# A decoder step whose first norm is summed on VectorE alone, behind two weight tiles, with its product four blocks later

## The chip, the cores and the metric

One core of a Trainium2 chip runs one launch of the whole step. The metric is the device time of that launch in microseconds (us), the median of several runs. The engines are TensorE (PE in the profile, with its weight loads shown as PEld), VectorE (DVE), ScalarE (ACT), GpSimd (POOL) and SyncE (SP), which here issues nearly all DMAs. Each engine works through its own instructions in the order in which they stand in its queue; semaphores tie the queues together.

## The reference

Two layers of a decoder, for a prompt of 256 positions and eight single-token samples. These 264 columns go through everything together.

```python
def rmsnorm(x, g):
    y = xf * lax.rsqrt(jnp.mean(xf * xf, axis=-1, keepdims=True) + EPS)
    return (y * g).astype(x.dtype)

def moba_gmlp_mixer(x, pos, past_kv, norm_g, w_in, ...):      # layer 0
    h = rmsnorm(x, norm_g)
    z = h @ w_in
    q, k, v, bu, bv = jnp.split(z, ...)
    ...
```

Layer 0 is followed by a ConvFFN, layer 1 by another, and a last rmsnorm ends the step. Only the start of layer 0 is touched here: the first rmsnorm and the product with `w_in`.

## The kernel before

Everything is kept transposed: features on the 128 partitions, the 264 columns along the free axis. A matrix product is made of **blocks** of 128x128 weights, and each block takes three TensorE matmuls, since weights and activations are split into a rounded high half (`wh`, `xg_h`) and a low half (`wl`, `xg_l`): high by high, high by low, low by high. All weights of the step are one stream of blocks in the order of their use. Eight blocks make one **weight tile**: tile n holds the blocks 8n to 8n+7, so tile 4 holds blocks 32 to 39, tile 5 blocks 40 to 47, tile 8 blocks 64 to 71. For each tile ScalarE writes the high half (`wh<-raw`, 128x1024) and VectorE the low half (`wl<-raw,wh`). The raw weights arrive by DMA in **chunks**: the first three tiles come together with `x` in `xw`, chunks 3, 4 and 5 are one tile each (tiles 3, 4, 5), and from chunk 6 on a chunk is two tiles of 1 MB in all (chunk 6 is tiles 6 and 7, chunk 7 tiles 8 and 9, chunk 8 tiles 10 and 11). Raw chunks from 6 on share three buffers, `wh` and `wl` have four each.

The norm is not applied ahead of the product: `z` is computed from `x` times the gain, and the factor R = rsqrt(mean square + eps) of each column is multiplied in when a finished output leaves its PSUM bank. To get R, ScalarE squares the eight slices of `x` into two tiles `sq0[0]` and `sq0[1]` of four slices; `sum0` folds each of them to one slice with two additions (128x528, then 128x264); one more addition (`summed`) joins the two; a TensorE product with a matrix of ones (`ns_n`) sums over the partitions; and ScalarE takes logarithm and exponential (`R_n`, in `rstd_of`). In the kernel before, GpSimd folds `sq0[0]` and VectorE `sq0[1]`.

The first product of layer 0, `in0`, has 20 outputs. The first six (four of `bv`, two of `q`) are accumulated side by side in blocks 0 to 47, the others one after the other with eight blocks each: q2 in blocks 48 to 55, q3 in 56 to 63, k0 in 64 to 71. Products take PSUM banks from a pool of four in turn (`psm`); q0, q1 and q2 (blocks 4, 5 and 48) take theirs from another pool. So q3, at block 56, takes the bank of the first `bv`, and k0, at block 64, that of the second. An output that is finished before R exists is put on a list (`held`), and `norm0`, which makes R, writes out those held.

The order of instructions comes from two sources. What goes through `keep` (`tc.keep_in_program_order`) stays in the order of the program on its engine: the start of the program, all TensorE work, and all of SP's loads through `late`. The rest is placed by a scheduler; `behind(i, j)` only tells it that instruction i comes after j. In the main loop `run`, `split(t)` prepares weight tiles up to three ahead (two for a few) and asks for the raw chunks of the tile and of the two chunks after it; `blk(b, f)` runs the hook f once b blocks have been written. `kload` hooks at blocks 24, 32, 40 and so on each put two loads of the sample's key cache (`K`, 256 KB each) into SP's queue. `whole(tt)` prepares a tile ahead of that loop, and does not ask for further chunks; the next call of `split` goes on from the first tile that isn't there yet.

Of the kernel before, what the change touches and what calls it, by code (L numbers as in the profile page):

```python
# [207 lines left out]
def tile_decoder_step(ctx: ExitStack, tc: tile.TileContext, a):  # L208
    nc = tc.nc
    v, s, g = nc.vector, nc.scalar, nc.gpsimd  # L210
    fixed = [False]

    class TensorE:

        @staticmethod
        def keep(i):
            return tc.keep_in_program_order(i) if fixed[0] else i
# [21 lines left out]
    def f4(name, shape=(P, 4, T), dt=F32):  # L239
        return up.tile(list(shape), dt, tag="u", name=name)  # L240
# [46 lines left out]
    def wtiles(tt):  # L287
        return [p.tile([P, 8, WP], F32R, tag=f"w{x}", name=f"w{x}{tt}")[:, :, :P] for p, x in ((wsh, "h"), (wsl, "l"))]

    def by_block(w):  # L290
        return w.rearrange("p (b c) -> p b c", c=P)

    def raw(ci):
        if ci not in raws:
            n = _CHUNKS[ci] * P
            r = f4(f"raw{ci}", (P, n)) if ci < C8 else rawp.tile([P, n], F32, tag="raw", name=f"raw{ci}")
            o = (coff[ci] - NB1) * P * P
            raws[ci] = r
            late(r, a["w"][o:o + P * n].rearrange("(p f) -> p f", p=P))
        return raws[ci]  # L300
# [7 lines left out]
    def split(t):  # L308
        for tt in range(len(splits), min(t + (2 if t in NEAR else LOOK), NT - 1) + 1):
            ci = chunk_of[tt]  # L310
            for c in range(ci, min(ci + 3, len(_CHUNKS))):
                raw(c)
            o = (tt * 8 - coff[ci]) * P
            src = by_block(raws[ci][:, o:o + 8 * P])
            h, l = splits[tt] = wtiles(tt)
            i = s.activation(h, src, AF.Copy)  # L316
            if R0 and tt < 9:
                behind(i, last[0])
            if tt == 17:
                behind(i, turned["a", 3])  # L320
            if tt == 18:
                behind(i, turned["t", 3])
            i = v.tensor_tensor(l, src, h.bitcast(F32), ALU.subtract)  # L323
            if tt == 5:
                behind(i, summed)
            if tt == 13:
                behind(i, turned["k", 1])
            if tt in (15, 16):
                behind(i, turned["p", 2 * tt - 29])
        return splits[t]  # L330
# [3 lines left out]
    def run(order, rhs, evac, hooks=None):  # L334
# [5 lines left out]
        for m, k in order:  # L340
            i = pos[0]
            pos[0] += 1
            h, l = split(i // 8)
            c = i % 8
            if m not in ps:
# [122 lines left out]
    def behind(i, j):  # L468

        tc.add_manual_dep(i.ins, j.ins.name, mybir.DependencyInfo(mybir.DependencyClass.NoSync, mybir.DependencyReason.DATA), reason="order")  # L470
# [275 lines left out]
    def whole(tt, pieces=1):  # L746
        h, l = splits[tt] = wtiles(tt)
        ci = chunk_of[tt]
        o = (tt * 8 - coff[ci]) * P
        src = by_block(raws[ci][:, o:o + 8 * P])  # L750
        n = 8 // pieces
        for c in range(0, 8, n):
            keep(s.activation(h[:, c:c + n], src[:, c:c + n], AF.Copy))  # L753
            keep(v.tensor_tensor(l[:, c:c + n], src[:, c:c + n], h[:, c:c + n].bitcast(F32), ALU.subtract))  # L754
# [10 lines left out]
    sq0 = [f4(f"sq0_{i}") for i in range(2)]  # L765
# [4 lines left out]
    def square(m):  # L770
        keep(s.activation(sq0[m // 4][:, m % 4, :], xin[m], AF.Square))
# [18 lines left out]
    def sum0(e, q):  # L790

        keep(e.tensor_tensor(q[:, 0:2, :], q[:, 0:2, :], q[:, 2:4, :], ALU.add))
        keep(e.tensor_tensor(q[:, 0, :], q[:, 0, :], q[:, 1, :], ALU.add))

    sum0(g, sq0[0])
    whole(4, 2)
    square(4)
    keep(s.activation(sq0[1][:, 1:4, :], first[-1][2], AF.Square))
    sum0(v, sq0[1])
    summed = keep(v.tensor_tensor(sq0[1][:, 0, :], sq0[0][:, 0, :], sq0[1][:, 0, :], ALU.add))  # L800
    rope = f4("rope")
    held = []
# [214 lines left out]
    blk = lambda b, f, *x: hk.at(b / 8 - 1, f, *x)  # L1017
# [12 lines left out]
        blk(112 + 6 * n, drip_of(vload, 2))  # L1030
    for m in range(0, KD, 2):
        blk(120 + 4 * m, late_x, m)
    blk(39, norm0)
    blk(40, masks)
    blk(44, gm_first)
    blk(64, late, VEC, a["vec"])
    blk(72, sm_q)
    for t in range(4):
# [205 lines left out]
    blk = lambda b, f, *x: hk.at(b / 8 - 1, f, *x)  # L1244
# [109 lines left out]
```

## Time and profile before

| what | value |
|---|---|
| median of 3 runs | 584.74 us (584.72 to 584.82) |
| the profiled execution's own time | 584.81 us |
| its span, first to last instruction | 583.0 us |
| granted TensorE clock, mean | 0.999 |
| busy: PE, DVE, ACT, POOL | 577.8, 421.7, 345.9, 113.3 us |
| DMA moved | 122.40 MB, mean 210 GB/s |

Times in the trace are counted from the start of the span; 1.8 us of the execution lie around it. A row of the timeline gives start, duration, engine, line, operation and tiles, with the number of merged instructions (x2) and, in square brackets, the idle time before it and who ended it. Buffer numbers are left out there, so that all weight tiles read `wl<-raw,wh`.

### The profile page before, as it was taken

To read this page: it belongs to the slowest core of one execution; us is meant where nothing else is said; L and a number is where in the kernel's file an instruction comes from. 1 tells how busy PE (TensorE), PEld (TensorE's weight loads), DVE (VectorE), ACT (ScalarE), POOL (GpSimd) and SP (SyncE) were. 2 spreads that over 40 slices of the span, in tenths; PEclk is the share of its full clock that TensorE was granted. 3 is DMA by queue.
4 is the path that set the end of the run, shared out by engine and by line. 5 is a ranking of instruction groups with operands and counts; after the bars stand their busy time and mean duration, and the time that the engine had idled before them with its cause. 6 is when DMAs were issued, how large, how long until landed. Compare 5 with 4: busy or idle time off the path is not lost.

```text
span 583.0 us, 12325 instructions
## 1 busy us (share of the span) xinstructions
PE 577.8 (99%) x4913; PEld 563.5 (97%) x4913; DVE 421.7 (72%) x743; ACT 345.9 (59%) x618; POOL 113.3 (19%) x108
## 2 busy tenths in 40 slices
PE   9999999999999999999999999999999999999997
PEld 8998979999999999999999897999999999999996
DVE  6999766877777777665659685688777777765442
ACT  7848945775555556654454576667656564665442
POOL 2410031222223232210110000122232323221010
PEclk9999999999999999999999999999999999999999
DMA  8998973455554545795567855254545454546501
GB/s 332 373 358 285 402 256 114 178 183 180 164 198 156 205 153 209 266 399 209 183 230 270 307 203 182 83 208 155 207 149 211 148 209 153 200 171 223 209 4 74
DMA packets 27707, 122.40 MB, mean 210 GB/s; under 512 B 3330, under 2 KB 4226, under 8 KB 16258
## 3 DMA queue, kind: packets, MB, share of 16 engines
q1 hardware_dynamic: 27648, 121.62, 58.3%
q8 instruction: 38, 0.62, 0.4%
q14 instruction: 19, 0.16, 0.1%
q10 hardware_dynamic: 2, 0.00, 0.0%
HBM read 117.65 MB, written 3.96 MB: 209 GB/s over the span
## 4 chain that ended last, share of the span: by engine, by line
PE 96%; ACT 1%; DMA 1%; DVE 1%; SPq 0%; issue 0%; DVEq 0%
PE mm L220 88%; PE sc L220 1%; PE pv_l L220 1%; PE pav L220 1%; PE pt L223 1%; DMA xw<-in_xw 1%; PE S L220 1%; PE Z L220 1%; DVE wl L754 0%; ACT xg_h L424 0%; PE pf L220 0%; PE vtp_v L223 0%; SPq L389 0%; ACT wh L753 0%; ACT wh L741 0%; PE y L223 0%
## 5 line engine op out<-in xcount | busy, mean ns | idle before, releaser
L323 DVE TENSOR_TENSOR wl<-raw,wh 128x1024 fp32r<-128x1024 f32 x179 | 219.5, 1230 | 63.8 <-ACT wh L316 63.5
L316 ACT ACTIVATE wh<-raw 128x1024 fp32r<-128x1024 f32 x179 | 187.7, 1051 | 79.6 <-PE mm L220 73.8
L220 PE MATMUL mm<-xg_f_h,wh 128*128 128x264 f32 x704 | 197.8, 281 | 0.0
L220 PE MATMUL mm<-xg_f_h,wl 128*128 128x264 f32 x704 | 197.8, 281 | 0.0
L220 PE MATMUL mm<-xg_f_l,wh 128*128 128x264 f32 x704 | 197.5, 280 | 0.0
L220 PEld LDWEIGHTS mm<-xg_f_h,wh 128*128 128x128 f32 x704 | 131.9, 187 | 0.0
L220 PEld LDWEIGHTS mm<-xg_f_h,wl 128*128 128x128 f32 x704 | 131.9, 187 | 0.0
L220 PEld LDWEIGHTS mm<-xg_f_l,wh 128*128 128x128 f32 x704 | 131.9, 187 | 0.0
L616 POOL TENSOR_TENSOR wk<-wk 128x264 f32<-128x264 f32 x44 | 66.5, 1513 | 193.5 <-DVE wk L615 147.3
L220 PE MATMUL mm<-a_h,wl 128*128 128x264 f32 x352 | 98.9, 281 | 0.0
L220 PE MATMUL mm<-a_h,wh 128*128 128x264 f32 x352 | 98.9, 281 | 0.0
L220 PE MATMUL mm<-a_l,wh 128*128 128x264 f32 x352 | 98.7, 280 | 0.0
L220 PEld LDWEIGHTS mm<-a_l,wh 128*128 128x128 f32 x352 | 66.0, 187 | 0.0
L220 PEld LDWEIGHTS mm<-a_h,wl 128*128 128x128 f32 x352 | 65.9, 187 | 0.0
L220 PEld LDWEIGHTS mm<-a_h,wh 128*128 128x128 f32 x352 | 65.9, 187 | 0.0
L473 ACT ACTIVATE a_h<-wk 128x264 fp32r<-128x264 f32 x44 | 18.6, 423 | 73.6 <-POOL wk L616 73.6
L474 DVE TENSOR_TENSOR a_l<-wk,a_h 128x264 fp32r<-128x264 f32 x44 | 19.2, 437 | 42.1 <-ACT a_h L473 42.1
L220 PE MATMUL mm<-xg_h,wl 128*128 128x264 f32 x160 | 42.7, 289 | 0.0
L220 PE MATMUL mm<-xg_h,wh 128*128 128x264 f32 x160 | 42.3, 286 | 0.0
L220 PE MATMUL mm<-xg_l,wh 128*128 128x264 f32 x160 | 41.6, 281 | 0.0
L220 PE MATMUL mm<-xg_n_h,wl 128*128 128x264 f32 x128 | 36.9, 288 | 0.0
L220 PE MATMUL mm<-xg_n_h,wh 128*128 128x264 f32 x128 | 36.0, 281 | 0.0
(271 smaller groups left out, 903.8 us busy)
## 6 DMA issues: line engine op xcount, KB each, us to landing
raw<-in_w SPq DMA_DIRECT2D x89, 1024.0 KB, 4.9
K<-in_kt SPq DMA_DIRECT2D x32, 256.0 KB, 7.0
V<-in_vp SPq DMA_DIRECT2D x32, 256.0 KB, 5.9
raw<-in_w SPq DMA_DIRECT2D x3, 512.0 KB, 6.6
xw<-in_xw SPq DMA_DIRECT2D x3, 388.0 KB, 5.4
X<-in_x SPq DMA_DIRECT2D x4, 264.0 KB, 6.9
out_y<-y SPq DMA_DIRECT2D x3, 256.0 KB, 2.3
out_k<-k SPq DMA_DIRECT2D x1, 528.0 KB, 7.5
```

The source lines that it names most:

```text
L220: return self.keep(nc.tensor.matmul(*x, **k))
L223: return self.keep(nc.tensor.transpose(*x, **k))
L316: i = s.activation(h, src, AF.Copy)
L323: i = v.tensor_tensor(l, src, h.bitcast(F32), ALU.subtract)
L473: s.activation(h, src, AF.Copy)
L474: v.tensor_tensor(l, src, h.bitcast(F32), ALU.subtract)
L616: g.tensor_tensor(A, A, C, ALU.mult)
```

## The change

Tile 4 is split in one piece instead of two. Tile 5 is now split with `whole` as well, ahead of the main loop, and after it VectorE does all the additions of the first norm, in the order `sq0[0]`, `sq0[1]`, `summed`. What the scheduler is told to keep behind `summed` is now the low half of tile 6 instead of tile 5. The hook with the norm's product and R moves from after 39 blocks to after 43, the masks from 40 to 44, the first gelu from 44 to 47.

```diff
             i = v.tensor_tensor(l, src, h.bitcast(F32), ALU.subtract)
-            if tt == 5:
+            if tt == 6:
                 behind(i, summed)
...
-    sum0(g, sq0[0])
-    whole(4, 2)
+    whole(4)
     square(4)
     keep(s.activation(sq0[1][:, 1:4, :], first[-1][2], AF.Square))
-    sum0(v, sq0[1])
+    whole(5)
+    for q in sq0:
+        sum0(v, q)
     summed = keep(v.tensor_tensor(sq0[1][:, 0, :], sq0[0][:, 0, :], sq0[1][:, 0, :], ALU.add))
...
-    blk(39, norm0)
-    blk(40, masks)
-    blk(44, gm_first)
+    blk(43, norm0)
+    blk(44, masks)
+    blk(47, gm_first)
```

Lines after the edit move down by one. In the rows below, numbers tell buffers apart within one kernel and differ between the two.

VectorE's queue from tile 4 on. In the kernel before, `wl_350` is tile 4, `wl_427`, `wl_487` and `wl_491` are tiles 5, 6 and 7; `mm_370` and `mm_380` are the accumulators of the first `bv` and of q0.

```order
L754 TENSOR_TENSOR wl_350<-raw_136,wh_349 128x4x128 x2
L792 TENSOR_TENSOR sq_1_312<-sq_1_312 128x528
L793 TENSOR_TENSOR sq_1_312<-sq_1_312 128x264
L800 TENSOR_TENSOR sq_1_312<-sq_0_311,sq_1_312 128x264
L323 TENSOR_TENSOR wl_427<-raw_157,wh_426 128x8x128
L323 TENSOR_TENSOR wl_487<-raw_159,wh_486 128x8x128
L323 TENSOR_TENSOR wl_491<-raw_159,wh_490 128x8x128
L807 TENSOR_TENSOR rope<-ropecs,R_n_517 128x264
L808 SCALAR_TENSOR_TENSOR rope<-ropecs,R_n_517 128x264
L841 TENSOR_TENSOR bv_366<-mm_370,R_n_517 128x264
```

In the changed kernel `wl_354` is tile 5 (it stands just ahead of these rows, behind tile 4), `wl_485` and `wl_489` are tiles 6 and 7, `wl_522` is tile 8, and `mm_372` and `mm_382` are the accumulators of the first `bv` and of q0.

```order
L792 TENSOR_TENSOR sq_0_311<-sq_0_311 128x528
L793 TENSOR_TENSOR sq_0_311<-sq_0_311 128x264
L792 TENSOR_TENSOR sq_1_312<-sq_1_312 128x528
L793 TENSOR_TENSOR sq_1_312<-sq_1_312 128x264
L801 TENSOR_TENSOR sq_1_312<-sq_0_311,sq_1_312 128x264
L323 TENSOR_TENSOR wl_485<-raw_159,wh_484 128x8x128
L323 TENSOR_TENSOR wl_489<-raw_159,wh_488 128x8x128
L323 TENSOR_TENSOR wl_522<-raw_480,wh_521 128x8x128
L834 STREAM_SHUFFLE rz_q_555<-mm_382 128x264
L808 TENSOR_TENSOR rope<-ropecs,R_n_536 128x264
L809 SCALAR_TENSOR_TENSOR rope<-ropecs,R_n_536 128x264
L842 TENSOR_TENSOR bv_368<-mm_372,R_n_536 128x264
```

Five additions instead of three now stand between tile 5's low half and tile 6's, and tile 8's low half and a shuffle stand ahead of everything that uses R.

ScalarE's queue, from tile 6 on. Before, with `wh_486` and `wh_490` for tiles 6 and 7, `wh_537` and `wh_582` for tiles 8 and 9:

```order
L316 ACTIVATE wh_486<-raw_159 128x8x128
L316 ACTIVATE wh_490<-raw_159 128x8x128
L462 ACTIVATE R_n_517<-ns_n_515,epst 128x264
L463 ACTIVATE R_n_517<-R_n_517 128x264
L817 ACTIVATE onesr<-ones 128x128
L819 ACTIVATE mask_361<-CST 128x127 x2
L316 ACTIVATE wh_537<-raw_424 128x8x128
L960 ACT_TABLE_LOAD
L316 ACTIVATE wh_582<-raw_424 128x8x128
```

In the changed kernel, with `wh_484`, `wh_488`, `wh_521` and `wh_580` for tiles 6, 7, 8 and 9:

```order
L316 ACTIVATE wh_484<-raw_159 128x8x128
L316 ACTIVATE wh_488<-raw_159 128x8x128
L316 ACTIVATE wh_521<-raw_480 128x8x128
L462 ACTIVATE R_n_536<-ns_n_534,epst 128x264
L463 ACTIVATE R_n_536<-R_n_536 128x264
L818 ACTIVATE onesr<-ones 128x128
L820 ACTIVATE mask_363<-CST 128x127 x2
L961 ACT_TABLE_LOAD
L316 ACTIVATE wh_580<-raw_480 128x8x128
```

Tile 8's high half has moved from behind R and the masks to a place ahead of R's logarithm.

SP's queue after the last register load. Before, with `raw_424` for chunk 7 (tiles 8 and 9) and `raw_484` for chunk 8:

```order
L282 DMA raw_424<-in_w 128x2048
L282 ISA
L282 DMA K_0_454<-in_kt 128x512
L282 ISA
L282 DMA K_0_454<-in_kt 128x512
L282 ISA
L282 DMA K_2_481<-in_kt 128x512
L282 ISA
L282 DMA K_2_481<-in_kt 128x512
L282 DMA raw_484<-in_w 128x2048
```

In the changed kernel, with `raw_480` for chunk 7 and `raw_482` for chunk 8:

```order
L282 ISA
L282 DMA K_0_450<-in_kt 128x512
L282 ISA
L282 DMA K_0_450<-in_kt 128x512
L282 ISA
L282 DMA K_2_477<-in_kt 128x512
L282 ISA
L282 DMA K_2_477<-in_kt 128x512
L282 DMA raw_480<-in_w 128x2048
L282 DMA raw_482<-in_w 128x2048
```

Chunk 7 was asked for when the main loop first prepared tile 5; with tile 5 done ahead of that loop, it is asked for with tile 6, after the hooks of blocks 24 and 32 have put four `K` loads into the queue. TensorE's matmuls stay as they were, but for the product `ns_n`, which stands four blocks later.

## The prediction

> **What bounds the kernel now.** I read the page first: the span, the busy times and the chain that ended last.
>
> ```profile
> span 583.0 us, 12325 instructions
> PE 577.8 (99%) x4913; PEld 563.5 (97%) x4913; DVE 421.7 (72%) x743; ACT 345.9 (59%) x618; POOL 113.3 (19%) x108
> PE 96%; ACT 1%; DMA 1%; DVE 1%; SPq 0%; issue 0%; DVEq 0%
> ```
>
> TensorE is busy for 99% of the span and carries 96% of the chain. A change can therefore win only the microseconds in which TensorE pauses, and it loses whatever new pause it makes, since hardly anything later is idle enough to take a delay back. So I looked for the pauses at the place of the change: the waits of the first 80 us name one, the product of the norm, on TensorE's loads and on its matmuls.
>
> ```profile
> PEld ns_n L220 <- DVE sq L800: 0.4, 1, 0.4
> PE ns_n L220 <- DVE sq L800: 0.2, 1, 0.2
> ```
>
> TensorE's timeline there, matmul by matmul (start, duration):
>
> ```profile
> 18.62 0.28 PE L220 MATMUL mm<-xg_h,wl 128*128 128x264 f32 x1
> 19.09 0.71 PE L220 MATMUL ns_n<-sq,ones 128*128 128x264 f32 x2 [0.19 <-DVE sq L800]
> 19.45 0.48 PE L220 MATMUL mm<-xg_h,wh 128*128 128x264 f32 x1
> 19.77 0.28 PE L220 MATMUL mm<-xg_l,wh 128*128 128x264 f32 x1
> 20.25 0.37 PE L220 MATMUL mm<-xg_h,wl 128*128 128x264 f32 x1
> 20.46 0.28 PE L220 MATMUL mm<-xg_h,wh 128*128 128x264 f32 x1
> 25.87 0.28 PE L220 MATMUL mm<-xg_h,wl 128*128 128x264 f32 x1
> ```
>
> Count matmuls, three to a block: 18.62 is the last of block 38, 19.45 the first of block 39, 20.25 the last of block 40, 20.46 the first of block 41 and 25.87 the first of block 56. From 20.46 to 25.87 stand 45 matmuls in 5.41 us, so one takes 0.120 us and a block 0.361. Block 38 leaves TensorE free at 18.74; the product starts at 19.09. That is a pause of **0.35 us**. The product itself takes 0.36 to the next matmul, and that one holds the following back to 19.77, 0.20 more than its 0.12. At 20.25 to 20.46 another 0.09 is lost, by the low half of tile 5. Everything the change can win here is 0.35 + 0.09 = 0.44 us.
>
> **Step 1, the additions.** VectorE and GpSimd before:
>
> ```profile
> L754 DVE TENSOR_TENSOR wl<-raw,wh x2: 685/688/691, 13.2 to 13.8; 128x512 fp32r<-128x512 f32 x2
> L754 DVE TENSOR_TENSOR wl<-raw,wh x2: 1249/1469/1689, 14.6 to 16.2; 128x512 fp32r<-128x512 f32 x2
> 14.08 1.61 POOL L792 TENSOR_TENSOR sq<-sq 128x528 f32<-128x528 f32 x1 [11.11 <-ACT sq L771]
> 15.77 1.09 POOL L793 TENSOR_TENSOR sq<-sq 128x264 f32<-128x264 f32 x1
> 17.34 0.69 DVE L792 TENSOR_TENSOR sq<-sq 128x528 f32<-128x528 f32 x1
> 18.07 0.43 DVE L793 TENSOR_TENSOR sq<-sq 128x264 f32<-128x264 f32 x1
> 18.60 0.43 DVE L800 TENSOR_TENSOR sq<-sq,sq 128x264 f32<-128x264 f32 x1
> 18.96 4.05 DVE L323 TENSOR_TENSOR wl<-raw,wh 128x1024 fp32r<-128x1024 f32 x3
> ```
>
> The first two rows group the four halves of tiles 3 and 4 (min/median/max in ns). Two take 0.69 us, and the two that overlap GpSimd's additions 1.69 and 1.25: the collision costs VectorE 1.00 + 0.56 = 1.56 us, and the change removes it. It adds `sq0[0]`'s two additions to VectorE: by the starts above 0.73 for the first (17.34 to 18.07), and 0.36 for the second, whose successor need not wait for it (as 18.60 to 18.96). And it puts tile 5 ahead of them, which must wait for ScalarE:
>
> ```profile
> 16.02 1.04 ACT L316 ACTIVATE wh<-raw 128x1024 fp32r<-128x1024 f32 x1
> 17.56 2.00 ACT L316 ACTIVATE wh<-raw 128x1024 fp32r<-128x1024 f32 x2 [0.50 <-DMA raw<-in_w]
> 19.90 0.48 ACT L462 ACTIVATE R_n<-ns_n,epst 128x264 f32<-128x264 f32 x1 [0.34 <-PE ns_n L220]
> 20.42 0.42 ACT L463 ACTIVATE R_n<-R_n 128x264 f32<-128x264 f32 x1
> 32.44 1.21 DVE L323 TENSOR_TENSOR wl<-raw,wh 128x1024 fp32r<-128x1024 f32 x1
> 33.58 0.45 DVE L833 STREAM_SHUFFLE rz_q<-mm 128x264 f32<-128x264 f32 x1
> ```
>
> Tile 5's high half ends at 17.06, its place on ScalarE being the same as before. Its low half starts at 17.10 and holds VectorE 1.14 (the last two rows: 32.44 to 33.58), to 18.24. Then 0.73 + 0.36 + 0.73 + 0.53 + 0.43 for the five additions: the sum is there at 21.02, two microseconds later than the 19.03 of before. TensorE reaches the product's new place at 18.74 + 4 x 0.361 = 20.18 and waits until 21.08. The pause grows to 0.90, the 0.09 of tile 5 goes: **+0.46 us** at this place (0.90 - 0.35 - 0.09). Bounds: 0 if tile 5's high half came 0.5 earlier, +0.6 if the low half took the 1.35 mean of the 4.05 row.
>
> **Step 2, the queues behind it.** This is the step that decides. R's logarithm now stands on ScalarE behind tile 8's high half, and the outputs that use R on VectorE behind tile 8's low half. Tile 8 comes with chunk 7, which on SP now stands behind four `K` loads. SP before, with the time from issue to landing of the loads concerned (chunk 7, the four `K`, chunk 8):
>
> ```profile
> 16.44 0.33 SPq L282 DMA_DIRECT2D raw<-in_w  x1
> DMA to landing us min/median/max: 4.8/4.8/4.8
> 16.96 2.82 SPq L282 DMA_DIRECT2D K<-in_kt  x4
> DMA to landing us min/median/max: 5.1/5.2/5.4
> L282 SPq DMA_DIRECT2D K<-in_kt x4: 332/338/1207, 17.0 to 19.5; - x4
> 20.21 0.34 SPq L282 DMA_DIRECT2D raw<-in_w  x1
> DMA to landing us min/median/max: 6.9/6.9/6.9
> ```
>
> Chunk 7 was issued at 16.44, right after the register loads, and landed at 21.24. Now the four `K` go first, 0.33 earlier than before, and chunk 7 takes the place that chunk 8 had, 0.33 earlier too: 20.21 - 0.33 = 19.88. It lands 4.8 later, as before, at **24.7**. The same comes from the bytes: the fourth `K` of before, issued at 19.45, landed about 24.6 behind the same 2 MB. Bounds: 23.8 if the first `K` takes 0.33 instead of its 1.21 in that row; 26.8 if chunk 7 takes the 6.9 of chunk 8. The Trainium skill, DMA: Bandwidth & Descriptors, section "Anatomy of one DMA — SWDGE (gpsimd) path", puts a DMA at about 2.0 us plus its bytes at 436 GB/s, which for 1 MB is an estimate of 4.4 us, against the 4.8 of the row; the sum below would be 0.4 smaller. It is fitted on another path than SP's, and I keep the row.
>
> From 24.7 on all is in queue order. Chunk 6, landed at 17.37 in the trace, was taken up at 17.56, 0.19 later; so tile 8's high half runs from 24.9 to 25.94. Then logarithm and exponential, 0.52 + 0.42: R is there at 26.9. VectorE starts tile 8's low half at 25.98 and goes on at 27.12 with the shuffle, both `rope` rows and the first `bv`:
>
> ```profile
> 22.93 0.42 DVE L807 TENSOR_TENSOR rope<-ropecs,R_n 128x264 f32<-128x264 f32 x1
> 23.28 0.42 DVE L808 SCALAR_TENSOR_TENSOR rope<-ropecs,R_n 128x264 f32<-128x264 f32 x1
> 23.62 1.44 DVE L841 TENSOR_TENSOR bv<-mm,R_n 128x264 f32<-128x264 f32 x4
> 24.99 0.45 DVE L833 STREAM_SHUFFLE rz_q<-mm 128x264 f32<-128x264 f32 x1
> 25.34 0.41 DVE L835 SCALAR_TENSOR_TENSOR q<-mm,rope 128x264 f32<-128x264 f32 x1
> ```
>
> Shuffle 0.35 and `rope` 0.35 + 0.34 put the first `bv` at 28.16; it ends 0.42 later, 28.58. Block 56 needs that `bv`'s PSUM bank. Before, the bank was free at 24.04 and block 56 came at 25.87: 1.8 us of cover. Now TensorE reaches block 56 at 26.33 (25.87 + 0.46) and waits until **28.62**.
>
> **The sum.** Block 56 starts 28.62 - 25.87 = 2.75 us later; the +0.46 of step 1 is inside it, so step 1 costs nothing of its own. Behind it: the other `bv` follow 0.34 apart, while the next bank is needed 2.9 later; tile 8 is ready long before block 64. Tile 9's low half stood at 27.85 before; now the 4.54 by which the first `bv` is later, less the 1.14 and 0.35 already done, make it 3.05 later, 30.9, and it is needed at block 72, 28.62 + 16 x 0.361 = 34.4. Tile 10's ended at 33.65 against a need at 34.53 (25.87 + 24 x 0.361); this 0.88 shrinks by 0.30 to 0.58. No further pause. The masks and the gelu move with R on ScalarE, under TensorE's delay. The profiled execution took 584.81 us, 0.07 above the median 584.74 of the runs, so the sum is set against the median: 584.74 + 2.75 = 587.5. With a landing between 23.8 and 26.8 it is +1.85 to +4.85.
>
> **Rivals.** A: chunk 7 is in time and step 2 costs nothing. R's chain needs 3.92 us from the landing to block 56, so this takes a landing by 26.33 - 3.92 = 22.4, 2.5 us after the issue; the fastest row is 4.8. Then only step 1 remains, 585.2, or, if the sums are in time too, -0.44, 584.3. For it speaks that the DMA queues were slack at 17 to 19:
>
> ```profile
> 17.00:18.00 1.00, 1.00 (x10) 1.00 (x10) 1.00 (x2) 0.50 (x2) 0.00 (x0) 1.00 0.79 125
> 18.00:19.00 1.00, 0.90 (x8) 0.69 (x6) 0.86 (x4) 1.00 (x2) 0.00 (x0) 1.00 0.75 295
> ```
>
> (The last two columns are the DMA share and GB/s.) But the slack lies before chunk 7 is issued. 8%.
>
> B: the delay runs on. VectorE is full from here to 60, and GpSimd's additions for `bv` again collide with low halves; each such collision costs up to the 1.00 above, and tile 10 has 0.58 to give. Two collisions instead of one overrun it by about 0.5 to 1: 588.3. 14%.
>
> C: the pause slows TensorE's clock. The granted clock (third column from the end above) stays 1.00 over a pause of 0.35, and no row shows one of 2.3. Were it halved for as long as the pause, that costs 1.15: 588.6. 7%. The Trainium skill, TensorE: Matmul & The Clock Gate, section "What's actually happening", wants an idle window of about 3.4 us before it halves the clock; by that rule it does not happen.
>
> D: a real gain, over 0.2%. Only 0.44 us of pause exists here, so it needs a rearrangement further on that I do not see: 583.5. 3%.
>
> **The numbers.** The forecast has the remaining 68%. About 0.2% (1.2 us) is what a measurement of this kernel can tell from no change: D is faster, A the same, all else slower. The range runs from 586.3 (landing at 23.5, a little below its lower bound) to 589.2 (the upper bound, with part of B or C); A, D and the worst of B and C lie outside.
>
> **What would show it.** TensorE pauses some 0.9 us at the product, and some 2.3 us at block 56, released by VectorE's `bv`. ScalarE waits for the DMA of `raw` some 5 us ahead of tile 8's high half, and R's logarithm starts near 26. The halves of tiles 3 and 4 all run without collision. I am wrong if chunk 7 lands before 23, if `bv` is not what block 56 waits for, or if another pause of over half a microsecond stands behind it.

## The result, and the profile after

The changed kernel takes 591.74 us (median of 5 runs, 590.71 to 592.57), the kernel before 584.82 on the same chip (584.72 to 585.12): a ratio of 1.012, 95% interval 1.0108 to 1.0131, or **+6.9 us**. The profiled execution is the slowest of the five, 592.57 us with a span of 590.8; against the profiled execution of before that is +7.8.

The page of the changed kernel: span, busy times, the chain by engine, and the clock granted to TensorE by slices of the span.

```profile
span 590.8 us, 12321 instructions
PE 580.9 (98%) x4913; PEld 566.7 (96%) x4913; DVE 421.1 (71%) x744; ACT 345.7 (59%) x617; POOL 111.3 (19%) x106
PE 94%; SPq 3%; DMA 1%; issue 1%; DVE 1%; ACT 0%; DVEq 0%; ACTq 0%
PEclk9979999999999999999999999999999999999999
```

TensorE executes the same 4913 matmuls, but is busy for 3.1 us more, and the clock has a dip in the third slice (29.5 to 44.3 us) that was not there before. The waits between 10 and 60 us name the pause and what led to it:

```profile
PE mm L220 <- DVE bv L842: 4.4, 1, 4.4
PE ns_n L220 <- DVE sq L801: 0.5, 1, 0.5
ACT wh L316 <- DMA raw<-in_w: 7.9, 2, 7.2
DVE wl L323 <- ACT wh L316: 4.8, 1, 4.8
```

VectorE's timeline from tile 3 on, in the changed kernel (rows between the additions and tile 8, and behind them, left out):

```profile
13.55 1.29 DVE L754 TENSOR_TENSOR wl<-raw,wh 128x512 fp32r<-128x512 f32 x2
15.34 1.23 DVE L754 TENSOR_TENSOR wl<-raw,wh 128x1024 fp32r<-128x1024 f32 x1 [0.49 <-ACT wh L753]
17.36 1.23 DVE L754 TENSOR_TENSOR wl<-raw,wh 128x1024 fp32r<-128x1024 f32 x1 [0.79 <-ACT wh L753]
18.50 0.70 DVE L792 TENSOR_TENSOR sq<-sq 128x528 f32<-128x528 f32 x1
20.79 0.43 DVE L801 TENSOR_TENSOR sq<-sq,sq 128x264 f32<-128x264 f32 x1
28.28 1.23 DVE L323 TENSOR_TENSOR wl<-raw,wh 128x1024 fp32r<-128x1024 f32 x1 [4.78 <-ACT wh L316]
30.66 1.44 DVE L842 TENSOR_TENSOR bv<-mm,R_n 128x264 f32<-128x264 f32 x4
```

The collisions with GpSimd are gone (the two halves of tile 3 take 1.29 together, tiles 4 and 5 1.23 each), and the sum is there at 21.22. Then VectorE stands still for 4.8 us ahead of tile 8's low half, and the first `bv` starts at 30.66 instead of 23.62: **7.0 us late**. ScalarE and SP show why:

```profile
17.94 2.01 ACT L316 ACTIVATE wh<-raw 128x1024 fp32r<-128x1024 f32 x2 [0.61 <-DMA raw<-in_w]
27.19 1.06 ACT L316 ACTIVATE wh<-raw 128x1024 fp32r<-128x1024 f32 x1 [7.25 <-DMA raw<-in_w]
28.15 0.46 ACT L462 ACTIVATE R_n<-ns_n,epst 128x264 f32<-128x264 f32 x1
```

```profile
16.99 2.49 SPq L282 DMA_DIRECT2D K<-in_kt  x4
19.52 1.20 SPq L282 DMA_DIRECT2D raw<-in_w  x2
L282 SPq DMA_DIRECT2D raw<-in_w x1: 432/432/432, 19.5 to 19.5; - x1
DMA to landing us min/median/max: 7.6/7.6/7.6
```

Chunk 7 is issued at 19.52 behind the four `K` loads and lands 7.6 us later, at 27.1 (the last two rows are the answer for that one load). ScalarE waits for it 7.25 us, with R's logarithm in the queue behind it although the product was done at 22. On TensorE, the last matmul of block 55, the first of block 56 and its successors, and the place where their distance changes again:

```profile
26.45 0.28 PE L220 MATMUL mm<-xg_h,wh 128*128 128x264 f32 x1
31.14 0.59 PE L220 MATMUL mm<-xg_h,wl 128*128 128x264 f32 x1 [4.41 <-DVE bv L842]
31.52 0.42 PE L220 MATMUL mm<-xg_l,wh 128*128 128x264 f32 x1
31.74 0.42 PE L220 MATMUL mm<-xg_h,wh 128*128 128x264 f32 x1
...
36.80 0.35 PE L220 MATMUL mm<-xg_l,wh 128*128 128x264 f32 x1
36.99 0.28 PE L220 MATMUL mm<-xg_h,wh 128*128 128x264 f32 x1
37.11 0.28 PE L220 MATMUL mm<-xg_h,wl 128*128 128x264 f32 x1
```

Block 56 starts at 31.14, 5.27 later than before. From there a matmul comes every 0.22 us instead of 0.12, until 36.8. The table by stretches has the clock behind the busy times (then DMA share and GB/s):

```profile
30.00:31.00 1.00, 0.00 (x0) 0.00 (x0) 1.00 (x3) 0.99 (x2) 0.11 (x1) 0.55 1.07 453
31.00:36.00 5.00, 4.86 (x22) 4.86 (x23) 5.00 (x11) 4.46 (x4) 2.55 (x3) 0.50 0.73 279
36.00:38.00 2.00, 2.00 (x15) 2.00 (x15) 2.00 (x8) 1.18 (x2) 0.68 (x1) 0.77 0.78 246
```

The clock is at 0.50 for some 6.8 us (0.9 us of the first row, all of the second, 0.9 us of the third). By the count of matmuls it costs 26 x 0.10 = 2.6 us, and 5.27 + 2.6 = 7.9 is about the 7.8 by which this execution is longer. At block 72 TensorE is 8.0 us late (39.62 against 31.60 before), and nothing behind it adds to that. Whether those 2.6 us are also what a steady clock would give back is another question; the fourth group of experiments asks it.

### The profile page after: what moved, and what is told of

It reads as the page before. It is cut to its first block, busy times and chain, and to the rows that moved or that the text cites. A ratio compares the mean times of both kernels' runs of the same rounds, so it can differ in the third digit from the quotient of the medians.

```text
span 590.8 us, 12321 instructions
## 1 busy us (share of the span) xinstructions
PE 580.9 (98%) x4913; PEld 566.7 (96%) x4913; DVE 421.1 (71%) x744; ACT 345.7 (59%) x617; POOL 111.3 (19%) x106
## 4 chain that ended last, share of the span: by engine, by line
PE 94%; SPq 3%; DMA 1%; issue 1%; DVE 1%; ACT 0%; DVEq 0%; ACTq 0%
PE mm L220 87%; DMA raw<-in_w 1%; PE sc L220 1%; PE pv_l L220 1%; SPq L379 1%; PE pav L220 1%; PE pt L223 1%; SPq L282 1%; SPq L389 1%; PE Z L220 1%; PE S L220 1%; PE pf L220 0%; PE vtp_v L223 0%; PE y L223 0%; PE pm L220 0%
## 5 line engine op out<-in xcount | busy, mean ns | idle before, releaser
L220 PE MATMUL mm<-xg_h,wl 128*128 128x264 f32 x160 | 44.4, 300 | 4.4 <-DVE bv L842 4.4
L220 PE MATMUL mm<-xg_h,wh 128*128 128x264 f32 x160 | 43.7, 295 | 0.0
L220 PE MATMUL mm<-xg_l,wh 128*128 128x264 f32 x160 | 43.0, 290 | 0.0
```

Source lines behind the costliest of these rows:

```text
L220: return self.keep(nc.tensor.matmul(*x, **k))
```

## Experiments

**Theory 1** is the prediction's step 2: R stands on ScalarE behind tile 8, and tile 8 waits for a chunk that SP asks for behind four `K` loads; both are needed for the loss. Rivals: **1b**, the late chunk hurts by itself, whatever R does; **2**, the additions on VectorE or the later product are the cost.

### Undoing one half of the cause

`e1_chunk7_first` puts chunk 7 back ahead of the `K` loads and leaves all else changed:

```diff
     whole(5)
+    raw(7)
```

> The changed kernel, with chunk 7 asked for right behind tile 5, ahead of the four K loads, as before the change; tile 8's high half stays ahead of R's logarithm on ScalarE. Theory 1 (R waits on ScalarE behind tile 8, and tile 8 for a late chunk 7): the chunk lands near 21.3 to 22, R is there by 24, block 56 does not pause, TensorE's clock stays at 1.00, and the time is 584.8 to 586. Theory 2 (the additions on VectorE and the later product are the cost, whatever the chunk does): it stays above 590.

Measured: 585.55 us (584.99 to 586.04) beside 585.13 of before, ratio 1.0008 (0.9998 to 1.0017). In its trace chunk 7 lands 4.9 us after its issue at 16.57, and R follows:

```profile
16.57 0.33 SPq L282 DMA_DIRECT2D raw<-in_w  x1
DMA to landing us min/median/max: 4.9/4.9/4.9
21.59 1.06 ACT L316 ACTIVATE wh<-raw 128x1024 fp32r<-128x1024 f32 x1 [0.95 <-DMA raw<-in_w]
22.55 0.46 ACT L462 ACTIVATE R_n<-ns_n,epst 128x264 f32<-128x264 f32 x1
```

`e2_tile8_behind_R` leaves chunk 7 late and lets tile 8 be prepared one step later, so that R comes ahead of it on ScalarE:

```diff
-    NEAR = (3, 10, 12, 15)
+    NEAR = (3, 5, 10, 12, 15)
```

> The changed kernel, with tile 8 prepared one step later in the main loop (at block 48 in place of 40), so that its halves stand behind R on ScalarE and VectorE; chunk 7 stays behind the four K loads and lands late, near 27. Theory 1: R at 23, no pause at block 56; tile 8's low half ends near 29.5, just when block 64 needs it; 585 to 586. If the lateness of chunk 7 alone costs the time (theory 1b), TensorE pauses some 4 us at block 64 in place of 56, and the time is above 589. Theory 2: above 590.

Measured: 586.31 us (585.41 to 587.46), ratio 1.0028 (1.0015 to 1.0040). That is a little above the expected 585 to 586. Chunk 7 is still late, it lands 6.3 us after its issue at 19.72, but block 56 no longer waits for what hangs on it:

```profile
22.15 0.48 ACT L462 ACTIVATE R_n<-ns_n,epst 128x264 f32<-128x264 f32 x1 [2.23 <-PE ns_n L220]
26.10 2.01 ACT L316 ACTIVATE wh<-raw 128x1024 fp32r<-128x1024 f32 x2 [1.12 <-DVE bv L842]
```

Either mend alone takes away most of the 6.9 us: by the ratios 0.5 (e1) and 1.6 (e2) are left. That is theory 1, and it refutes 1b. `e3_both` has both edits:

> The changed kernel with both mends: chunk 7 ahead of the K loads, and tile 8's halves behind R. Theory 1: no pause at block 56, tile 8 long in time; what is left is the product's wait for five additions, 0.3 to 0.9 us, against the 0.44 us of before: 584.9 to 585.8, the same as with the first mend alone.

It took 585.89 us (585.63 to 586.08), ratio 1.0014 (1.0004 to 1.0023): the two are two ways out of one loss, and don't add (expected were 584.9 to 585.8).

### The parts by themselves

`e8_norm_later` is the kernel before with only the hooks moved, `e7_sums_only` the kernel before with only the additions moved, and `e4_norm_at_39` the changed kernel with the hooks back:

```diff
e8, on the kernel before:
-    blk(39, norm0)
-    blk(40, masks)
-    blk(44, gm_first)
+    blk(43, norm0)
+    blk(44, masks)
+    blk(47, gm_first)
e7, on the kernel before:
-    sum0(g, sq0[0])
...
-    sum0(v, sq0[1])
+    for q in sq0:
+        sum0(v, q)
e4, on the changed kernel:
-    blk(43, norm0)
-    blk(44, masks)
-    blk(47, gm_first)
+    blk(39, norm0)
+    blk(40, masks)
+    blk(44, gm_first)
```

> The kernel before, with the three hooks at 43, 44 and 47 and nothing else. Tile 8 then stands ahead of R, but chunk 7 keeps its early place on SP and lands near 21.3. Theory 1: the product need not wait (sum ready at 19.0, needed at 20.2), R at about 23.5, first bv near 24.8, block 56 at 25.5 without a pause: 584.3 to 584.8, no slower than before. Theory 2 (a later product costs time by itself): slower by 1.5 or more.

> The kernel before with one part of the change alone: both sums on VectorE (GpSimd's two additions gone), everything else where it was, tile 5 in the main loop, the product at 39. If the additions cost nothing once chunk 7 and tile 8 keep their places: 584.7 to 585.4, as before; the sum comes some 0.5 us earlier or later than the 19.03 of before, which moves the product's pause of 0.35 by as much. Rival: the additions on VectorE are themselves a cost of about a microsecond (1.1 us more work ahead of the sum against 1.56 of collisions less): 585.8 to 586.3.

> The changed kernel with the three hooks back at 39, 40 and 44. Tile 8 is then prepared after R and stands behind it, while chunk 7 stays late. Theory 1: the product waits at block 39 for the additions, from 18.7 or 19.2 to 21.1, a pause near 2 us, R at 22.8, no other pause and no slower clock: about 586.5 to 587. Theory 1b (the late chunk alone): above 590. Theory 2: 587, too, so this run does not tell 1 from 2.

Measured: e8 585.27 us, ratio 1.0006 (0.9997 to 1.0016); e7 584.60, ratio 0.9995 (0.9986 to 1.0004), with no pause at the product; e4, expected at 586.5 to 587, 587.79, ratio 1.0044 (1.0027 to 1.0061). So neither the additions nor the later product costs anything measurable, and theory 2 falls. What costs is tile 5 ahead of the loop, by way of chunk 7, together with R set too late to hold tile 8 back: in `split` a tile below 9 goes behind R on ScalarE only if R has been made when the tile is prepared, and tile 8 is prepared at block 40.

e4 showed something else. TensorE waits for the sum there, and behind a pause of 2.1 us the clock fell (waits, then the table by stretches):

```profile
PE ns_n L220 <- DVE sq L801: 2.1, 1, 2.1
22.00:23.00 1.00, 1.00 (x6) 1.00 (x5) 1.00 (x2) 0.73 (x2) 0.00 (x0) 0.50 0.91 309
25.00:26.00 1.00, 1.00 (x10) 1.00 (x10) 1.00 (x5) 0.00 (x0) 0.00 (x0) 1.00 1.03 434
```

The dip lasts from 21.5 to 24.9. TensorE is 2.12 us late at the first matmul of block 39 (21.57 against 19.45 before) and 3.54 late at block 56 (29.41 against 25.87), and the whole execution is 3.53 longer: here the 1.4 us of slow matmuls went through to the end.

### Why the chunk took 7.6 us

The prediction had 4.8. Three runs vary what stands around chunk 7 on SP:

```diff
e6, chunk 7 between the second and the third K load:
+    blk(25, raw, 7)
     blk(43, norm0)
e9, eight register loads on SP right behind chunk 7:
             late(r, a["w"][o:o + P * n].rearrange("(p f) -> p f", p=P))
+            if ci == 7:
+                pause_sp()
e11, late, but ahead of the K loads, behind five register loads:
     whole(5)
+    pause_sp(5)
+    raw(7)
```

> The changed kernel with chunk 7 behind two K loads in place of four. Theory 1: chunk 7 is issued near 18.5 and lands about 1.1 us earlier than in the changed kernel, near 25 to 26; the pause at block 56 shrinks by as much, to about 3 us, and the time lies between, 587.5 to 590.5. If what counts is only whether tile 8 stands ahead of R, and not when its chunk lands, it stays at 591.7.

> The changed kernel with eight idle register loads (0.57 us each) on SP between the loads of chunk 7 and chunk 8, so that chunk 7 has the DMA queues almost to itself. Theory A (chunk 7 took 7.6 us in place of 4.8 because chunk 8 and the K loads issued right behind it share the queues with it): it lands 4.6 to 5 us after its issue, near 24.4, the pause at block 56 falls to 1.5 to 2.3 us, and the time to 587 to 589 by the clock's part. Theory B (it is slow whatever stands behind it): 7 us or more, 591 or more. Chunk 8 comes 4.6 us later, to 30 or 31, and tile 10, for block 80, may then be tight.

> Why chunk 7 took 6.3 to 7.6 us instead of 4.8. Here it is asked for ahead of the four K loads, but behind five more register loads on SP (about 0.6 us each), so that it leaves as late as in the changed kernel, near 19.5, with no K load ahead of it. If the K loads ahead of it are the reason: it lands 4.8 to 5.0 us after its issue, near 24.5, block 56 waits about 2.1 us, and with a clock at half for some 3.4 us behind that pause the time is 587.8 to 588.8. If every such load at this time takes 6.3 to 7.6, whatever stands ahead: it lands at 26 to 27 and the time is 590 to 592, as the changed kernel.

e6 took 587.81 us (587.10 to 590.67), ratio 1.0048 (1.0028 to 1.0068), in between. e9 took 591.03, ratio 1.0105 (1.0088 to 1.0122): with nothing issued behind it for 5 us, chunk 7 still took 7.0 us.

```profile
16.79 2.79 SPq L282 DMA_DIRECT2D K<-in_kt  x4
19.62 5.79 SPq L282 DMA_DIRECT2D raw<-in_w  x2
DMA to landing us min/median/max: 7.0/7.0/7.0
```

e11 issues it later still, at 20.09, but with no `K` ahead and four right behind, and it lands 4.7 us later:

```profile
20.09 0.34 SPq L282 DMA_DIRECT2D raw<-in_w  x1
DMA to landing us min/median/max: 4.7/4.7/4.7
24.94 1.06 ACT L316 ACTIVATE wh<-raw 128x1024 fp32r<-128x1024 f32 x1 [3.46 <-DMA raw<-in_w]
28.89 0.39 PE L220 MATMUL mm<-xg_h,wl 128*128 128x264 f32 x1 [2.12 <-DVE bv L848]
```

So the `K` loads ahead of it are the reason, not those behind it, and not the later time of its issue. The Trainium skill, DMA: Bandwidth & Descriptors, section "Queues, rings and completion order", says that each of the sixteen DMA engines takes up the descriptors of a queue in order; the trace agrees, 4.7 against 7.0 us. e11 took 588.93 us (588.45 to 589.26), ratio 1.0069 (1.0055 to 1.0083). It shows one thing more: its chunk lands at 24.8, where the prediction put it, its block 56 starts at 28.89 where the prediction said 28.62, and yet the whole costs 3.9 us, not 2.75. Of its five executions the two with a mean clock of 0.999 and 1.000 cost 3.4 and 3.6, the three with 0.995 or 0.996 cost 3.9 to 4.2.

### What the clock costs, and the second gate

Four kernels ask what the 2.6 us at half clock are worth. Two fill TensorE's pause with matmuls on ones that nothing reads (`e5_fill`, 20 of them at block 56, behind R's logarithm; `e10_fill_bank_free`, 34 ahead of block 55, waiting for nothing), `e15_late_no_k_fill` does so in e11 with 17. `e13_fill_later_pt` and `e14_later_pt` move the attention's first transposes (`pt`) in e10 and in the changed kernel.

```diff
e5:
+            pe.matmul(bank_of["n0"][:1, T:T + 240], unit[0], unit[1][:, :240], start=True, stop=True, skip_group_check=True)
...
+    blk(56, fill, 20)
e10 (34) and e15 (17):
+            tc.keep_in_program_order(pe.matmul(bank_of[48][:1, T:T + 240], unit[0], unit[1][:, :240], start=False, stop=False, skip_group_check=True))
...
+    blk(55, fill, 34)
e13 and e14:
-    for h, b in enumerate((113, 113, 120, 121, 133, 133, 140, 140)):
+    for h, b in enumerate((118, 118, 120, 121, 133, 133, 140, 140)):
```

> The changed kernel with 20 extra matmuls of ones on TensorE just ahead of block 56; they write an unused part of the norm product's bank, and start when R's logarithm has read it. The pause of 4.4 us at block 56 is then broken into one of about 2 us, 2.2 us of extra work, and a rest. Theory: the clock's fall to 0.5 (26 matmuls at 0.22 us in place of 0.12) comes from the length of the pause, and block 56 still starts near 31; with the extra work the clock stays up or falls for one stretch of about 3.4 us in place of two, and the time is 589 to 590.5, 1 to 2.6 below the changed kernel. Rival (the pause alone costs all 6.9 us, the clock nothing): no change from 591.7.

e5 took 591.73 us (590.35 to 592.57), ratio 1.0115 (1.0098 to 1.0132), not the expected 589 to 590.5. Its filling begins only behind R, and the clock stayed up in one of four runs, the fastest, so it decided little.

> The clock's part, taken alone. 34 TensorE matmuls of 1x240 on ones (0.11 us each by the earlier fill, 3.8 us in all) stand just ahead of block 55 and wait for nothing, so that TensorE works through most of the 4.4 us for which block 56 waits. R, tile 8 and chunk 7 are untouched. If the pause of TensorE is what slows its clock: the granted clock stays 1.00 behind block 56, three matmuls take 0.36 us there, and the time falls by the 2.6 us put down to the clock, from 591.7 to about 589.1 (588.3 to 589.7), with block 56 still starting near 31. If the clock falls for another reason, or if the slow matmuls come from something else than the clock: 591 to 592.5, as the changed kernel.

e10 kept the clock at 0.999 or 1.000 in all four runs, and took **591.41 us** (590.50 to 591.97), ratio 1.0113 (1.0098 to 1.0129). The expected 589.1 was wrong: keeping the clock up in this way gained nothing that could be measured. Its trace has the filling, and then a wait that the changed kernel does not have:

```profile
25.54 3.71 PE L220 MATMUL mm<-const-bfloat16-1.0 128*1 128x240 bf16 x34
49.65 0.28 DVE L872 CUSTOM_DVE_ANT_0 p<-S,mask 128x128 f32<-128x128 f32 x1
52.98 1.06 PE L223 MATMUL pt<-CST,p 128*128 128x128 f32 x6 [1.04 <-DVE p L876]
```

Before, the same two steps, VectorE's first softmax of the attention and TensorE's first transposes of it, stood here:

```profile
44.66 0.27 DVE L866 CUSTOM_DVE_ANT_0 p<-S,mask 128x128 f32<-128x128 f32 x1
48.02 1.00 PE L223 MATMUL pt<-CST,p 128*128 128x128 f32 x6
```

From softmax to transposes are 3.36 us in the kernel before and 3.33 in e10, where the transposes follow VectorE's part of `p`, 1.00 us long there (51.93 to 52.93) instead of 0.26. Before, that part is done at 47.40; the second transpose starts at 48.18, right behind ScalarE's part of `p`, which ends at 48.13. So already before, TensorE came to `pt` without slack. VectorE, late with `bv`, has no idle time up to there; it catches up only what it has done ahead of `bv` this time, tile 8's low half and a shuffle (1.2 to 1.5 us in the kernels without filling).

The profiled executions, by their lateness against before (us; chunk 7 landed at 24.8 in e11, 24.7 in e15, 25.3 in e10, 26.6 in e9, 27.1 in the changed kernel):

| kernel | first `bv` | block 56 | block 72 | first softmax | `pt` | whole execution |
|---|---|---|---|---|---|---|
| e11, clock up | 4.80 | 3.03 | 3.14 | 3.61 | 3.42, and 0.2 lost behind it | 3.64 |
| e15, clock up by filling | 4.69 | 2.92 | 3.02 | 4.43 | 3.69, and 0.7 lost behind it | 4.51 |
| e10, clock up by filling | 5.27 | 3.77 | 3.78 | 4.99 | 4.96 | 5.69 |
| e9, clock fell | 6.55 | 4.78 | 6.19 | 5.36 | 6.19 | 5.93 |
| changed kernel, clock fell | 7.04 | 5.27 | 8.02 | 5.58 | 8.02 | 7.76 |

The table shows two different cases. Where the clock stayed up, TensorE waits, and goes on as late as the softmax is. Where it fell, TensorE comes to `pt` later than the softmax and waits for nothing there; its slow matmuls, the step from block 56 to block 72, go through to the end but for 0.3 us. An estimate from this: with a steady clock the changed kernel's execution would have left `pt` 5.58 late instead of 8.02, 2.4 us less, and that of e9 0.8 less.

Why, then, did filling gain nothing? It changed VectorE's queue too. The first two rows are the first softmax and the last addition for `k` in the changed kernel; the third is the same addition in e10, where it stands ahead of the softmax (49.65 above). The last row, the changed kernel's transposes, has no wait:

```profile
50.24 0.28 DVE L867 CUSTOM_DVE_ANT_0 p<-S,mask 128x128 f32<-128x128 f32 x1
52.32 0.42 DVE L840 TENSOR_TENSOR k<-k,rz_k 128x264 f32<-128x264 f32 x1
49.30 0.43 DVE L845 TENSOR_TENSOR k<-k,rz_k 128x264 f32<-128x264 f32 x1
56.04 0.82 PE L223 MATMUL pt<-CST,p 128*128 128x128 f32 x6
```

In all four filled kernels (e5, e10, e13, e15) the scheduler placed this addition and the product before it ahead of the softmax. From the first `bv` to the first softmax VectorE takes 20.8 us in each of them, and 19.6 to 19.9 in e9, e11, e14 and the changed kernel. So the filling costs about 0.9 us at `pt`, and these kernels do not show the clock's price alone.

> Where the time went that the clock should have given back. The kernel with the fill ahead of block 55 (591.41, clock 1.00 in every run, and a pause of 1.0 us at the first transposes of the attention, pt, released by VectorE's p) with those transposes, of heads 0 and 1, moved from after block 113 to after block 118, 1.8 us later on TensorE. If VectorE, late with the softmax because it was late with the first output, is the gate that takes the clock's gain: the pause at pt goes and the time falls by 0.6 to 1.5 us, to 590.0 to 590.8. If not: 591 to 592, with a pause elsewhere or the same time without one.

> The changed kernel with the same two sets of transposes after block 118 and nothing else. TensorE at half clock behind block 56 comes to pt later than VectorE in the profile (no pause there), so this should give nothing: 591.4 to 592.2, with the clock at 0.50 behind block 56 as before. Rival: in the executions that were not profiled TensorE waits at pt as well, and the time falls by half a microsecond or more, to 591.2 or less.

> The clock's own price where the landing is steady. The kernel with chunk 7 late but ahead of the K loads took 588.93; its five runs were 588.45 and 588.64 with a mean clock of 0.999 and 1.000, and 588.93 to 589.26 with 0.995. Here 17 matmuls of 1x240 (1.9 us) stand ahead of block 55 so that TensorE has no pause of 2.1 us there. If the clock's fall costs what those runs differ by: every run has a clock of 0.999 or 1.000 and the median is 588.4 to 588.7. If the runs differ for another reason (the landing): the clock is 1.000 and the median stays 588.8 to 589.2.

e15's clock was 0.998 to 1.000 in all five runs, and it took 589.32 us (589.12 to 589.74), ratio 1.0077 (1.0063 to 1.0091), no less than e11 with 588.93. The lateness stands in two waits at `pt`, behind the later softmax:

```profile
PE pt L223 <- ACT p L883: 0.6, 1, 0.6
PE pt L223 <- DVE p L882: 0.5, 1, 0.5
```

e13 took 590.89 us (589.97 to 593.41; 584.91 before, ratio 1.0117, 1.0099 to 1.0134). Its wait at `pt` shrank from 1.0 to 0.2 us, but small waits behind it took its place (5.16 late at the end, after 3.98 at block 72), and 0.5 us between medians whose runs overlap this much show no gain. e14 took 591.41 (590.04 to 592.99), ratio 1.0114 (1.0097 to 1.0132), the time of the changed kernel. **What stays open**: how much a steady clock alone would give back at the median. The 2.4 us are an estimate from the slowest of five executions, and no trace here shows a steady clock with the changed kernel's VectorE queue and its chunk behind the four `K` loads. Within e4, e5, e6, e11 and e14 the executions with a mean clock of 0.998 or more are the shortest (in e6 587.10 to 587.29, against 588.33 to 590.67 at 0.995 or 0.996), but the landing of chunk 7 may differ between them too.

### A version meant to win

`e12_norm_at_46` has chunk 7 first as e1, and the product after 46 blocks, masks after 47, the first gelu after 50:

> A version meant to win: the changed kernel with chunk 7 asked for ahead of the K loads, and the product three blocks later still (after 46 blocks, masks after 47, gelu after 50), where the sum should be ready. If the pause at the product is all that was left to win: no pause at the product, block 56 not waited for, and 0.3 to 0.5 us below the kernel with chunk 7 first (585.55), that is 585.0 to 585.3, the kernel before or a little under. Rival: R now comes so late that block 56 waits for the first output's bank by 0.3 to 1 us: 585.6 to 586.5.

It took 585.06 us, ratio 1.0000 (0.9991 to 1.0009). The pause at the product is gone, and block 56 waits 0.6 us for `bv` instead. No version here is measurably faster than the kernel before.

## Why the prediction was right and wrong

**What bounds, and the sign.** Right: TensorE carries the chain, and the loss begins at block 56, released by `bv`. The 0.44 us to be won are seen in e7's trace (block 39 starts at 18.96 instead of 19.45), but not in its time, 0.9995 of the kernel before.

**Step 1.** Right in its parts. The collisions went (1.29, 1.23 and 1.23 us), the sum was forecast for 21.02 and came at 21.22. The pause at the product was 0.66 by the prediction's way of counting (0.50 in the list of waits) instead of 0.90, since TensorE itself came there half a microsecond later than forecast (20.71, forecast 20.18). As forecast, this is inside the wait at block 56, and e1, which keeps this step and has no such wait, takes 1.0008 of the time before.

**Step 2, the order.** Right in every link: chunk 7 behind the `K` loads, tile 8 behind chunk 7, R behind tile 8, `bv` behind R, block 56 behind `bv`. From landing to block 56 the forecast had 3.92 us and the trace has 31.14 - 27.08 = 4.06.

**Step 2, the landing: the first step that failed.** "It lands 4.8 later, as before": issued at 19.52 (forecast 19.88) it took 7.6. The 4.8 was the row of the load in its old place, ahead of the `K` loads; the row of a load in its new place stood beside it, chunk 8's 6.9, and was used only as a bound, which the landing at 27.1 passed by 0.3. The second derivation, by bytes, took it that the same 2 MB land at the same time in any order; with the 1 MB load last they landed at 27.1 instead of 24.6. e11 and e9 show the price of the place: 4.7 without the `K` loads ahead, 7.0 with them. This moved block 56 from 28.62 to 31.14, 2.5 us. The range did not hold its own bound either: a landing at 26.8 gives 584.74 + 4.85 = 589.6, and the range ended at 589.2.

**The sum: the second step that failed.** It put everything behind block 56 at nothing ("No further pause"). In the changed kernel's profiled execution TensorE loses 2.7 us more there at half clock, from 5.27 late to 8.0. In e11, whose clock stayed up in the profile and whose landing was as forecast, it loses 0.6, 0.2 each by waits for VectorE's `k` at the scores (`S`) and for ScalarE's `p` at `pt`, the rest in smaller steps. "No further pause" was asked of the weight tiles alone, 9 and 10, and they were in time; the softmax, whose 3.36 us to `pt` stand in the trace of before without slack, was not asked. With the landing where it was forecast the change would have cost 3.9 us (e11's median), 1.2 above the sum.

**Rival C** was right in kind, thought too unlikely, and its price too simple. The clock did halve, behind pauses of 4.4 and of 2.1 us. The rule of the Trainium skill, TensorE: Matmul & The Clock Gate, section "What's actually happening", that the clock halves after an idle window of about 3.4 us, does not hold here for the pause itself: in e4 2.1 us were enough. The same section says that the window runs freely and isn't reset by the kernel; that agrees with e4 and e11, whose pauses of 2.11 and 2.12 us were followed by a clock of 0.50 and of 1.00. C had the clock halved for as long as the pause, at a price of half of it; the changed kernel's pause of 4.4 us was followed by a dip of 6.8 us, 1.0 of which lay in the pause, and cost 2.7.

**Rival B**, the delay running on, does not show in the changed kernel's trace: nothing collided at tile 10 by which TensorE had to wait. In e11 it is the 0.6 us above, by way of the scores and `pt`. **A** and **D** did not occur.

## What to carry to other kernels

Price a load that changes its place in a queue by the row of the load that stands in that place now, not by its own old row. When an output is late, follow the engine that makes it to its next idle time, and ask at each hand-over on the way how much slack the other engine had; the first buffer that comes free late is only the first gate. A slow clock or a pause that stands in a trace is worth no more than the slack behind it. And a filling that is meant to take it away is an edit like any other: compare the queues of the other engines before reading its time as the price.

## What the runs showed of the hardware

A pause of TensorE of 2.1 us can be followed by a clock of 0.50 for 3.4 us (e4, 21.5 to 24.9), one of 4.4 us by 6.8 us of it, which begins 1.0 us before the pause ends; at that clock a matmul of 264 columns comes every 0.22 us instead of 0.12. A pause of the same 2.1 us was also followed by none (e11), and matmuls of 1x240 in the pause kept the clock at 0.998 or more in every run of e10 and e15, and at 0.997 or more in e13. A load of 1 MB landed 4.7 to 5.3 us after its issue with no load of the cache ahead of it, and 6.0 to 7.6 us behind four loads of 256 KB, while what was issued behind it made no difference that could be seen (7.0 with nothing).
